# The GLA heads of a two-layer streaming step: SyncE's transfers in the source's order, the first gates and the samples' values asked later

## The chip, the core and the metric

The kernel runs on one core of one Trainium2 chip. The metric is the device time of one execution in microseconds (us). The core has five engines with a queue of instructions each, executed in order: TensorE (PE, matrix products), ScalarE (ACT), VectorE (DVE), GpSimd (POOL) and SyncE (SP), which only issues transfers. Transfers (DMA) are issued by SP, ACT and POOL and carried by 16 shared DMA engines; the profile names the queues of the three q1 (SP), q10 (ACT) and q0 (POOL). An instruction waits for semaphores that others raise, and whatever stands behind it on its engine waits too.

## The reference

Two layers act on 512 prompt frames and on 8 running streams of 16 frames each, 640 frames of 2048 channels together. The first is stick-breaking attention; the second, which matters here, is gated linear attention (GLA) with four heads. In float32, for chunks of a head:

```python
def gla_chunk(S, inp):
    q, k, v, g = inp
    C = q.shape[1]
    b = jnp.cumsum(g, axis=1)
    b_last = b[:, -1]
    q_in = q * jnp.exp(b)
    a = jnp.einsum('bchd,bshd->bhcs', q_in, k * jnp.exp(-b))
    a = jnp.where(jnp.tril(jnp.ones((C, C), dtype=bool)), a, 0.0)
    o = jnp.einsum('bhcs,bshe->bche', a, v) + jnp.einsum('bchd,bhde->bche', q_in, S)
    S = jnp.exp(b_last)[..., None] * S + jnp.einsum('bshd,bshe->bhde', k * jnp.exp(b_last[:, None] - b), v)
    return S, o

def gla_mixer(h, w_in, w_a2, b_a, g_out, w_out, S0=None):
...
    q, k, v, r, a_lr = jnp.split(h @ w_in, [nk, 2 * nk, 2 * nk + nv, 2 * nk + 2 * nv], axis=-1)
...
    g = (jax.nn.log_sigmoid((a_lr @ w_a2 + b_a).astype(f32)) / GLA_TAU).reshape(B, T, GLA_HEADS, GLA_DK)
...
    o = o * lax.rsqrt(jnp.mean(o * o, axis=-1, keepdims=True) + EPS) * g_out.astype(f32).reshape(GLA_HEADS, GLA_DV)
    y = (o.reshape(B, T, nv) * jax.nn.silu(r.astype(f32))).astype(h.dtype) @ w_out
    return y, S.astype(h.dtype)
```

For the streams S0 is the given state; the new states are outputs.

## The kernel before

Every float32 product is made of three reduced ones: a weight piece `wr` (128x1024, 512 KB) is cast by ACT to `wh` (L134) and the rest is subtracted by DVE to `wl` (L135), and PE multiplies wh, wh and wl with the two halves of the activations. Weights are read once, from HBM, with two raw buffers in flight, so a piece is asked for when ACT and DVE have emptied the buffer that it takes.

The change touches one stage, "layer 1's heads" (the block that opens at L1508). Five pieces of work run in it beside one another:

- `plain` (L632) makes q and k of heads 1 to 3 from the normed input: a unit is 48 matmuls of 128x320 with one weight piece, two units make a block of 128 channels, and `keep` (L1513) copies the block's two halves out of PSUM by ACT (`pl`, L1519) and stores it by ACT's queue to `gq` or `gk` in HBM (L1521). There are two PSUM banks for it, so a half can begin only when the copy of that half of the block before is done.
- `decays` loads a head's q and k back (`load`, L71, by SP) and makes the decay factors on ACT and DVE.
- `prompt_lane` runs 16 chunks (4 heads of 4): scores, the product with the values `v` (fetched two chunks ahead from `gv` in HBM, two pairs of buffers), the state S, the norm, and the multiplication by the output gate (`gate`, fetched from `gr`, GP buffers), whose result ACT stores to `og` (L1610). When that store is issued, the gate that will take the same buffer is asked after a delay.
- `sample_lane` does the streams: 64 states of 256 KB go in and out by POOL's queue (`move`, L78), and for every head its values are brought by SP (`v`) and POOL (`vst`).
- `fetches` loads the finished `og` rows back (`og_in`) and splits them; `share` (L686) multiplies them with the output weights, its first products copied out by ACT (`y`, L708) and later ones added by DVE (L705).

Which of these comes next is decided while the program is written: a planner counts PE's time ("pe now", in us) and steps the pieces; `side.after(t, f)` calls f when t us of PE's time have gone by. That gives the source's order. The order in which an engine's queue gets its instructions is then made by a scheduler, from times that it estimates, over all engines; only dependences bind it. So SP's transfers before the change stand in the scheduler's order and not in the source's. Each transfer of SP and ACT takes the next of eight semaphores in turn, and one that takes a semaphore waits until the transfer that had it before has landed.

Of the kernel before, what the change touches and what calls it, by code (L numbers as in the profile page):

```python
# [34 lines left out]
GP = 2  # L35
# [6 lines left out]
def hybrid_step_kernel(ctx: ExitStack, tc: tile.TileContext, A: dict, O: list):  # L42
# [106 lines left out]
    def wraw(src, a, n):  # L149
        r = wp.tile([P, 1024], F32, tag="wr", name="wr", bufs=WR)[:, :a * n]  # L150
        load(r.rearrange("p (a n) -> p a n", a=a), src)
        return r
# [121 lines left out]
    def step(wait=0.0, tp=0, z=0, tiled=False):  # L274
        return wait, tp, z, tiled
# [70 lines left out]
    side = Side()  # L346
# [569 lines left out]
    with tc.tile_pool(name="kp", bufs=2, reuse_waits="tile") as kp, \  # L916
# [297 lines left out]
        for x in (prompt_lane(0), prompt_lane(1), sample_lane()):  # L1214
            side.add(x)
# [287 lines left out]
    def w_of(g, c, i):  # L1503

        k0 = 4 * g + 2 * i
        return w_out1.rearrange("(kt p) n -> p kt n", p=P)[:, k0:k0 + 2, 512 * c:512 * c + 512]

    with tc.tile_pool(name="gl", bufs=1, reuse_waits="tile") as gl, \  # L1508
            tc.tile_pool(name="w4", bufs=1, reuse_waits="tile") as w4:
        came = {"plain": False, "last": False, "of": 0, "when": 0.0}  # L1510

        def keep(dst, hh):
# [78 lines left out]
        def gate(h, t0, tag, bufs):  # L1591
            g = gl.tile([P, 4, P], F32, tag=tag, name="gate", bufs=bufs)
            load(g, gr_d[h][:, :, t0:t0 + P])
            return g
# [7 lines left out]
        def leave(h, t0, on, g, then):  # L1602

            tp = bank("tp")
            for s in range(4):
                turn_block(tp[:, P * s:P * s + P], block(on[:, P * s:P * s + P]), ident)
            dve.tensor_tensor(g, tp.rearrange("p (s t) -> p s t", s=4), g, op=ALU.mult)

            def out():
                nc.scalar.dma_start(out=og_d[h][:, :, t0:t0 + P], in_=g)  # L1610
                then()
            side.after(2.0, out)
# [66 lines left out]
        def prompt_lane():  # L1679
# [7 lines left out]
            def fetch_gate(u):  # L1687
                if u < len(units):
                    gs[u] = gate(units[u][0], P * units[u][1], "gp", GP)
# [1 line left out]
            fetch(0)  # L1691
            side.after(10.0, lambda: fetch(1))
            for u in range(GP):
                side.after(14.0 + 2.0 * u, lambda u=u: fetch_gate(u))
            left = None

            def state(S, e1, dt, c):
# [7 lines left out]
            def leave_left():  # L1705
                nonlocal left
                u, on = left
                left = None
                h, c = units[u]

                def then():
                    side.after(7.0, lambda: fetch_gate(u + GP))
                    if c == 3:
                        through["p"] = h + 1
                leave(h, P * c, on, gs.pop(u), then)
# [94 lines left out]
        def sample_lane():  # L1810
            def fetch(h):
                v = values(h, 4, "vn", 1)

                for e in range(2):
                    for i in range(3):
                        rows = gv_d[h][int(i == 1)][NP:, :].rearrange("(m e t) n -> e t m n", m=4, e=2)[e]
                        r0 = 64 * e + NT * i
                        move(vst[r0:r0 + NT].bitcast(F32), rows)
                return v, gate(h, NP, "gn", 1)

            yield step(12.0)
            here = fetch(0)
            for h in range(GH):
                v, g = here
# [134 lines left out]
        for x in (decays(), prompt_lane(), sample_lane(), fetches()):  # L1959
            side.add(x)  # L1960
# [8 lines left out]
        parts = [split(r) for r in first]  # L1969
        first = [wraw(w_of(3, 0, i), 2, 512) for i in range(2)]  # L1970
        side.finish()


    share_banks(mm=8)
# [96 lines left out]
```

## Time and profile before

| | |
|---|---|
| median of three runs | 2514.42 us (2511.73 to 2514.44) |
| the profiled execution | 2514.76 us, its span 2513.0 us |
| mean granted clock of PE | 0.984 |
| the stage of the change | about 1979 to 2395 us of the span |
| PE's idle time before matmuls of `plain` (L654, wh) | 8.8 us, of it 6.3 for ACT's copy pl |
| transfers in the whole run | 503.12 MB, mean 200 GB/s |
| of it by SP, POOL, ACT | 441.85, 41.43 and 17.04 MB |

A row of a timeline has the start in the span (us), the length (us), the engine, the line of the kernel, the operation, out<-in by the program's names, the shape, how many instructions are drawn together, and in brackets how long the engine stood before it and what released it. SPq and ACTq are the issues of transfers on these engines: their length is that of the issue, or of the stretch over several, and not of the transfer. A row of waits has the engine and line, what it waited for, the us in total, how often, and the longest. A row of a DMA queue has its packets, MB and share of the 16 engines' time in the window. A row of the chain of waits has the start, the length and what the time went to.

The share of DMA time in the stage changes much: in windows of 20 us it is 1.01 from 1980 (303 GB/s), 0.66 from 2000, 0.54 from 2020, 1.00 from 2080, 0.49 from 2120 and 1.03 from 2240 (373 GB/s).

### The profile page before, as it was taken

To read this page: it belongs to the slowest core of one execution; us is meant where nothing else is said; L and a number is where in the kernel's file an instruction comes from. 1 tells how busy PE (TensorE), PEld (TensorE's weight loads), DVE (VectorE), ACT (ScalarE), POOL (GpSimd) and SP (SyncE) were. 2 spreads that over 40 slices of the span, in tenths; PEclk is the share of its full clock that TensorE was granted. 3 is DMA by queue.
4 is the path that set the end of the run, shared out by engine and by line. 5 is a ranking of instruction groups with operands and counts; after the bars stand their busy time and mean duration, and the time that the engine had idled before them with its cause. 6 is when DMAs were issued, how large, how long until landed. Compare 5 with 4: busy or idle time off the path is not lost.

```text
span 2513.0 us, 43986 instructions
## 1 busy us (share of the span) xinstructions
PE 2427.7 (97%) x17561; PEld 2150.1 (86%) x17561; DVE 1580.6 (63%) x2566; ACT 994.1 (40%) x1731; POOL 135.2 (5%) x350
## 2 busy tenths in 40 slices
PE   6899999999999999999999999999999999999998
PEld 4589999899999998888887767999999989987776
DVE  5575555555666655666776568766676466675556
ACT  4332222222223334555544245333333455565223
POOL 0010000000000000000000000000000212332000
PEclk8899999999999999999999999999999999999999
DMA  9966666667664357777874664443534758976634
GB/s 343 330 210 216 224 205 208 221 214 226 209 202 126 110 166 227 256 243 236 259 235 146 187 226 134 129 118 110 145 104 117 209 183 271 294 265 218 226 114 147
DMA packets 487502, 503.12 MB, mean 200 GB/s; under 512 B 42746, under 2 KB 387202, under 8 KB 487170
## 3 DMA queue, kind: packets, MB, share of 16 engines
q1 hardware_dynamic: 456978, 441.85, 55.8%
q0 software_dynamic: 12848, 41.43, 4.8%
q10 hardware_dynamic: 17472, 17.04, 2.0%
q8 instruction: 138, 2.26, 0.4%
q14 instruction: 66, 0.54, 0.1%
HBM read 411.10 MB, written 89.13 MB: 199 GB/s over the span
## 4 chain that ended last, share of the span: by engine, by line
PE 78%; DMA 6%; DVE 4%; ACT 3%; issue 1%; SPq 0%; POOL 0%; ACTq 0%; POOLq 0%; DVEq 0%
PE ps_mm L595 40%; PE ps_mm L700 9%; PE ps_mm L654 9%; PE ps_mm L369 3%; PE ps_tp L1086 2%; DMA gv<-kr 2%; PE ps_tp L1559 2%; PE ps_mm L519 1%; PE ps_tp L1046 1%; PE ps_tp L1138 1%; PE ps_z L1022 1%; PE ps_z L180 1%; PE ps_mm L2042 1%; PE ps_z L1100 1%; PE ps_z L222 1%
## 5 line engine op out<-in xcount | busy, mean ns | idle before, releaser
L595 PE MATMUL ps_mm<-sums,wh 128*128 128x320 f32 x2752 | 613.5, 311 | 1.5 <-ACT wh L134 1.5
L595 PE MATMUL ps_mm<-h,wh 128*128 128x320 f32 x2064 | 462.8, 312 | 4.7 <-DVE u L601 4.7
L595 PEld LDWEIGHTS ps_mm<-sums,wh 128*128 128x128 f32 x2752 | 457.9, 188 | 10.4 <-issue 7.4
L595 PE MATMUL ps_mm<-sums,wl 128*128 128x320 f32 x1376 | 425.3, 309 | 0.7 <-DVE wl L135 0.7
L135 DVE TENSOR_TENSOR wl<-wr,wh 128x1024 fp32r<-128x1024 f32 x193 | 236.1, 1224 | 232.3 <-ACT wh L134 228.9
L595 PEld LDWEIGHTS ps_mm<-h,wh 128*128 128x128 f32 x2064 | 344.0, 188 | 20.7 <-issue 14.6
L134 ACT CAST wh<-wb 128x1024 fp32r<-128x1024 f32 x170 | 178.4, 1050 | 426.5 <-PE ps_mm L595 350.3
L134 ACT CAST wh<-wr 128x1024 fp32r<-128x1024 f32 x193 | 202.5, 1050 | 329.3 <-PE ps_mm L595 186.7
L595 PE MATMUL ps_mm<-h,wl 128*128 128x320 f32 x1032 | 319.3, 309 | 0.0
L654 PE MATMUL ps_mm<-h,wh 128*128 128x320 f32 x1152 | 265.7, 318 | 8.8 <-ACT pl L1519 6.3
L595 PEld LDWEIGHTS ps_mm<-sums,wl 128*128 128x128 f32 x1376 | 258.3, 188 | 1.0 <-DVE wl L135 1.0
L135 DVE TENSOR_TENSOR wl<-wb,wh 128x1024 fp32r<-128x1024 f32 x170 | 207.8, 1223 | 62.7 <-ACT wh L134 62.5
L654 PEld LDWEIGHTS ps_mm<-h,wh 128*128 128x128 f32 x1152 | 193.7, 190 | 23.5 <-issue 8.9
L700 PE MATMUL ps_mm<-wh,ogh 128*128 128x512 f32 x450 | 197.3, 438 | 7.2 <-ACT y L708 4.0
L595 PEld LDWEIGHTS ps_mm<-h,wl 128*128 128x128 f32 x1032 | 194.2, 188 | 0.0
L654 PE MATMUL ps_mm<-h,wl 128*128 128x320 f32 x576 | 178.8, 310 | 0.0
L700 PE MATMUL ps_mm<-wl,ogh 128*128 128x512 f32 x450 | 177.2, 394 | 0.3 <-DVE wl L135 0.3
L700 PE MATMUL ps_mm<-wh,ogl 128*128 128x512 f32 x450 | 177.2, 394 | 0.3 <-DVE ogl L135 0.3
L700 PEld LDWEIGHTS ps_mm<-wh,ogh 128*128 128x128 f32 x450 | 85.0, 189 | 35.7 <-issue 14.3
L654 PEld LDWEIGHTS ps_mm<-h,wl 128*128 128x128 f32 x576 | 109.1, 189 | 0.2 <-DVE wl L135 0.2
L700 PEld LDWEIGHTS ps_mm<-wh,ogl 128*128 128x128 f32 x450 | 84.7, 188 | 20.3 <-DVE ogl L135 0.7
L519 PE MATMUL ps_mm<-wh,h 128*128 128x512 f32 x252 | 93.2, 431 | 5.7 <-ACT h L134 3.7
(359 smaller groups left out, 3712.9 us busy)
## 6 DMA issues: line engine op xcount, KB each, us to landing
ar<-in_w_ada_dram SPq DMA_DIRECT2D x160, 512.0 KB
wb<-in_sb_w_in_dram SPq DMA_DIRECT2D x82, 512.0 KB
kc<-in_cache_sb_k_dram SPq DMA_DIRECT2D x64, 512.0 KB
vc<-in_cache_sb_v_dram SPq DMA_DIRECT2D x64, 512.0 KB
wr<-in_gla_w_in_dram SPq DMA_DIRECT2D x51, 512.0 KB
wb<-in_gla_w_in_dram SPq DMA_DIRECT2D x45, 512.0 KB
wr<-in_sb_w_in_dram SPq DMA_DIRECT2D x44, 512.0 KB
ar<-in_w_ada_dram SPq DMA_DIRECT2D x64, 256.0 KB
```

The lines of the kernel that those rows point to most:

```text
L134: nc.scalar.copy(hi, x)
L135: (e or dve).tensor_tensor(lo, x, hi.bitcast(F32), op=ALU.subtract)
L180: mm(acc[32 * q:32 * q + 32, :w], cT[:, kt + m, :], by(cT[:, kt + m, :], rs[m // each][:, m % each, q, :]), start=kt + m == 0, stop=kt + m ...
L222: mm(acc[32 * j:32 * j + 32, :256], cT[:, kt + m, :], by(cT[:, kt + m, :], r[:, 256 * j:256 * j + 256]), start=kt + m == 0, stop=kt + m == ...
L369: mm(acc[a], l[:, c], by(l[:, c], r[:, k2, :]), start=kt == k0 and first, stop=kt == k0 + nk - 1 and last)
L519: mm(acc[a], l, by(l, r[:, e, :]), start=j == 0 and e == 0 and begun, stop=j == 7 and e == 1 and last)
L595: mm(acc, l[:, k, :], by(l[:, k, :], r), start=start and k == 0 and first, stop=k == 7 and last, skip_group_check=True)
L654: mm(acc[nt], l[:, k, :], by(l[:, k, :], r), start=k0 == 8 and k == 0 and first, stop=k0 == 0 and k == 7 and last)
L700: mm(acc, l, by(l, r[:, e, :]), start=i == 0 and e == 0 and first, stop=i == 1 and e == 1 and last)
L1022: mm(z[:, :n], q[:, hh, qs], by(q[:, hh, qs], k[:, hh, :n]), start=True, stop=True)
L1086: turn_block(tp[:, P * c:P * c + P], block(kc[:, c, P * hh:P * hh + P]), ident)
L1559: mm(out, l[a], by(l[a], r[b]), start=start and n == 0, stop=stop and n == 2, skip_group_check=True)
```

## The change

Four edits, all in the heads' stage:

- SP's queue is taken from the scheduler for the length of the stage (`manual_schedule` for the engine SP): its transfers are issued in the order in which the source asks for them. The other engines' queues are still the scheduler's.
- The first GP gates are asked at 40, 44, ... us of the planner's clock instead of 14, 16, ...
- A gate that refills a buffer is asked 6 us after the store that frees it, instead of 7.
- The samples' lane begins at 30 us instead of 12, and with it its values are asked later.

```diff
@@ -1507,6 +1507,8 @@
     with tc.tile_pool(name="gl", bufs=1, reuse_waits="tile") as gl, \
             tc.tile_pool(name="w4", bufs=1, reuse_waits="tile") as w4:
+        loads = ExitStack()
+        loads.enter_context(tc.manual_schedule(engines={mybir.EngineType.SP}))
         came = {"plain": False, "last": False, "of": 0, "when": 0.0}
@@ -1691,7 +1693,7 @@
             for u in range(GP):
-                side.after(14.0 + 2.0 * u, lambda u=u: fetch_gate(u))
+                side.after(40.0 + 4.0 * u, lambda u=u: fetch_gate(u))
@@ -1709,7 +1711,7 @@
                 def then():
-                    side.after(7.0, lambda: fetch_gate(u + GP))
+                    side.after(6.0, lambda: fetch_gate(u + GP))
@@ -1818,7 +1820,7 @@
-            yield step(12.0)
+            yield step(30.0)
             here = fetch(0)
@@ -1969,6 +1971,7 @@
         side.finish()
+        loads.close()
```

The rest is told by the order of the rows on each engine, in which a row is the line, the operation, out<-in and the shape. PE's rows stand in the same order before and after. Those of ACT, DVE and POOL move a little; POOL's moves `vst` keep their place among its transfers. SP's rows move much. Lines of the changed kernel are 2 higher in this stage.

The first place is the beginning of the stage on SP, from the first pair of values on, about 1982 us of the span; `-` is before and `+` the change:

```order
 L71 DMA v<-gv_0_107 128x512
 L71 DMA v<-gv_1_108 128x512
+L71 DMA wr<-in_gla_w_in_dram 128x8x128
 L71 DMA q<-gq_95 128x1280
 L71 DMA k<-gk_99 128x1280
+L71 DMA wr<-in_gla_w_in_dram 128x8x128
 L71 DMA v<-gv_0_107 128x512
 L71 DMA v<-gv_1_108 128x512
+L71 DMA wr<-in_gla_w_in_dram 128x8x128 x2
 L71 DMA v<-gv_0_107 128x512
 L71 DMA v<-gv_1_108 128x512
-L71 DMA gate<-gr_103 128x4x128 x3
```

Two weights that stood ahead of these rows now stand among them, two more came forward from behind the gates, and the three gates are now asked one by one, later.

The second place is SP about 2086 to 2102 us, before:

```order
L71 DMA gate<-gr_104 128x4x128
L71 DMA og_in<-og_91 128x384
L71 DMA wa_21838<-wa_d 96x256
L71 DMA wr<-in_gla_w_in_dram 128x8x128
L71 DMA gate<-gr_104 128x4x128
L71 DMA wr<-in_gla_w_in_dram 128x8x128
```

and now:

```order
L71 DMA gate<-gr_104 128x4x128
L71 DMA wr<-in_gla_w_in_dram 128x8x128
L71 DMA gate<-gr_104 128x4x128
L71 DMA wr<-in_gla_w_in_dram 128x8x128
L71 DMA wa_21840<-wa_d 96x256
L71 DMA wr<-in_gla_w_in_dram 128x8x128
```

The second gate is the same in both. The weight that stood ahead of it (with wa) now stands behind it, and the weight that is now ahead of it was asked earlier still, outside these rows.

The third place is about 2238 to 2262 us, where the output weights and the og rows are brought; SP before:

```order
L71 DMA wr<-in_gla_w_out_dram 128x2x512
L71 DMA og_in<-og_92 128x640
L71 DMA v<-gv_1_114 128x512
L71 DMA v<-gv_0_113 128x512
L71 DMA wr<-in_gla_w_out_dram 128x2x512
L71 DMA k<-gk_102 128x1280
L71 DMA og_in<-og_92 128x640 x2
L71 DMA gate<-gr_106 128x4x128 x2
L71 DMA og_in<-og_92 128x640
L71 DMA wr<-in_gla_w_out_dram 128x2x512 x2
```

and now:

```order
L71 DMA wr<-in_gla_w_out_dram 128x2x512 x2
L71 DMA q<-gq_98 128x1280
L71 DMA k<-gk_102 128x1280
L71 DMA og_in<-og_92 128x640 x2
L71 DMA gate<-gr_106 128x4x128
L71 DMA og_in<-og_92 128x640
L71 DMA gate<-gr_106 128x4x128
L71 DMA wr<-in_gla_w_out_dram 128x2x512 x2
```

q of the last head (asked near 2192 before) now stands here, and the weight that stood ahead of k is the first of the last row, behind both gates and three og rows.

ACT at the same place, about 2260 to 2268 us, before (the first row is the cast of that weight):

```order
L134 CAST wh<-wr 128x1024
L1651 ACTIVATE b<-b 128x640
L708 COPY y<-ps_mm 128x512
L1652 ACT_TABLE_LOAD
L1652 ACTIVATE b<-b 128x640
L1848 CAST kc<-kd 128x4x32
L1610 DMA og_93<-gate 512x1x128
L708 COPY y<-ps_mm 128x512
L1661 ACT_TABLE_LOAD
```

and now:

```order
L1612 DMA og_93<-gate 512x1x128
L708 COPY y<-ps_mm 128x512
L134 CAST wh<-wr 128x1024
L1663 ACT_TABLE_LOAD
L1663 ACTIVATE e_23482<-b 128x4
L1664 ACTIVATE el<-b 128x4
L1666 ACTIVATE es<-b 128x8
L1669 ACTIVATE ed<-ed 128x4
L708 COPY y<-ps_mm 128x512
```

The cast of the same weight has moved from ahead of the second decay's steps to between the copy and the table load, with the next copy y six rows behind it.

## The prediction

> **What bounds the kernel now.** First the page, for the share of TensorE (PE), then PE's waits in the stage that the change touches, 1960 to 2400 us of the span.
>
> ```profile
> PE 2427.7 (97%) x17561; PEld 2150.1 (86%) x17561; DVE 1580.6 (63%) x2566; ACT 994.1 (40%) x1731; POOL 135.2 (5%) x350
> ```
> ```profile
> PE ps_mm L654 <- ACT pl L1519: 6.3, 1, 6.3
> PE ps_mm L700 <- ACT y L708: 3.8, 2, 1.9
> ```
>
> PE is busy 97% of the span, so only its waits can be won, and in this stage they are few: 6.3 us once, for a copy of ScalarE (ACT) that frees a bank, and 3.8 us in two waits for other copies of ACT. PE's own order is the same before and after; the change acts only through the loads of SyncE (SP). The ACT timeline and the chain of waits show where the 6.3 us come from.
>
> ```profile
> 1986.96 1.05 ACT L134 CAST wh<-wr 128x1024 fp32r<-128x1024 f32 x1 [1.12 <-PE ps_mm L654]
> 1990.63 0.43 ACT L1519 COPY pl<-ps_mm 128x320 f32<-128x320 f32 x1 [2.62 <-PE ps_mm L654]
> ...
> 2002.59 0.33 ACTq L1521 DMA_DIRECT2D gq<-pl  x1
> 2002.95 1.28 ACT L1651 ACT_TABLE_LOAD   x1 [7.00 <-DMA v<-gv]
> ```
> ```profile
> 1986.01 16.50 DMA v<-gv
> ```
>
> ACT stood 7.00 us until a load of values (issued 1986.01, 16.50 us under way) had landed. What waited was the store gq<-pl at the head of its queue: the eight semaphores of SP's and ACT's transfers go round, and the one that the store got was held by that load. Behind it stood the decays and the copy that PE wanted. The PE timeline gives the price.
>
> ```profile
> 2015.08 0.90 PE L654 MATMUL ps_mm<-h,wh 128*128 128x320 f32 x2 [6.26 <-ACT pl L1519]
> ...
> 2018.38 0.45 PE L654 MATMUL ps_mm<-h,wh 128*128 128x320 f32 x2
> 2018.82 0.46 PE L654 MATMUL ps_mm<-h,wh 128*128 128x320 f32 x2
> ```
>
> PE stood 6.26 us. The 12 matmuls from 2015.08 to 2018.38 then took 3.30 us; three take 0.44 us at the full clock (2018.38 to 2018.82), so 1.76 us: 1.54 us more are lost to the slower clock. **The place costs 7.8 us in all.**
>
> The other side of the stage is its transfers. Of the DMA view I read three windows: 1983 to 1997 (its row of SP's queue, q1), 2089 to 2102 (GpSimd's queue q0, then q1) and 2239 to 2255 (q1).
>
> ```profile
> q1 hardware_dynamic: 865, 2.28, 52.8%
> ```
> ```profile
> q0 software_dynamic: 825, 2.56, 60.5%
> q1 hardware_dynamic: 1615, 0.97, 24.7%
> ```
> ```profile
> q1 hardware_dynamic: 1101, 2.62, 45.8%
> ```
>
> Beside GpSimd's states SP's queue moved 2.28 MB in 14 us (0.163 MB/us) and 2.62 MB in 16 us (0.164) where it held long packets too, but 0.97 MB in 13 us (0.075) where it held mostly short ones, as a weight is. These are my two prices for a load that has to land in such a stretch.
>
> **The change part by part.** *The store (−7.8).* In the new order the store's semaphore belongs to the first pair of values, asked some 2 us earlier and with far less ahead of them; ACT's wait of 7.00 us goes, and the 6.26 and 1.54 us with it. What is late next is a weight. SP's timeline:
>
> ```profile
> 1967.31 10.89 SPq L71 DMA_DIRECT2D wr<-in_gla_w_in_dram  x3
> 1978.63 3.08 SPq L74 DMA_DIRECT2D gr<-out  x2
> 1981.81 0.37 SPq L71 DMA_DIRECT2D alr_in<-alr_d  x1
> 1982.23 0.43 SPq L71 DMA_DIRECT2D wa<-wa_d  x1
> 1982.71 1.84 SPq L71 DMA_DIRECT2D v<-gv  x2
> ```
>
> *Third and fourth weight (+5.4).* Before, three weights were asked by 1978.2. Now one is; the next (cast at 1986.96 before) follows the two v, at about 1984.6, into GpSimd's burst of states. Ahead of its end in SP's queue, from 1981.4: one gr 320, alr 240, wa 96, two v 512 and itself 512, 1.68 MB. At 0.163 MB/us from 1983 it lands at 1993.3; with its own 512 KB at 0.075 at 1997.0. I take the middle, 1995.2. Then the cast (1.05) and VectorE's subtraction, by its group on the page:
>
> ```profile
> L135 DVE TENSOR_TENSOR wl<-wr,wh 128x1024 fp32r<-128x1024 f32 x193 | 236.1, 1224 | 232.3 <-ACT wh L134 228.9
> ```
>
> 1.22 us. It is usable at 1997.5, and ACT's copy of 1990.63, which stands behind that cast, is late too. PE wants both when the unit that began at 1986.9 ends: 48 matmuls of 0.147 us and two of the decays, 1994.2. PE stands 3.0 us (0 to 5). The fourth weight follows q and k (1.28 MB): 1.79 MB more at 0.163 would be 2006.2, somewhat sooner as the states end near 2000; usable about 2006.8, against 1994.2 + 3.0 + 7.2 = 2004.4: 2.4 us (0 to 4). Net of this first place: −7.8 + 5.4 = **−2.4** (−7.8 to +1).
>
> *First gates, samples' values, delay of 6.0: nothing.* GpSimd's moves of the samples' values keep their place in its order, so that part hardly exists. The gates' cover is long:
>
> ```profile
> 2052.74 1.03 SPq L71 DMA_DIRECT2D v<-gv  x2
> 2056.61 0.54 SPq L71 DMA_DIRECT2D gate<-gr  x1
> ```
> ```profile
> 2060.27 1.05 ACT L134 CAST wh<-wr 128x1024 fp32r<-128x1024 f32 x1 [0.17 <-PE ps_mm L654]
> ```
>
> The gate of 2056.61 refills the buffer of the first one used, so that one was used just before; asked up to 25 us later it is still there 20 us ahead. Without that cover every us late would be a us of VectorE's queue.
>
> *Weights behind values, 2050 to 2090 (+2, 0 to 6) and 2140 to 2230 (+1.5, 0 to 5).* In source order a weight stands behind the pair of values asked before it, which waits until PE has freed their buffers. So the weight of the cast of 2060.27 is asked at 2053.8, behind the pair of 2052.74; its 512 KB take 3.1 to 6.8 us and some start, so ACT may wait 0 to 2 us with PE's copy behind it. The same once more near 2086, and at some four weights later; most keep several us of slack.
>
> *Behind a gate (+4, 0 to 9).*
>
> ```profile
> 2088.48 0.55 SPq L71 DMA_DIRECT2D wr<-in_gla_w_in_dram  x1
> 2101.44 0.54 SPq L71 DMA_DIRECT2D gate<-gr  x1
> 2102.07 0.65 SPq L71 DMA_DIRECT2D wr<-in_gla_w_in_dram  x1
> ```
> ```profile
> 2102.60 1.05 ACT L134 CAST wh<-wr 128x1024 fp32r<-128x1024 f32 x1 [1.04 <-PE ps_mm L654]
> 2103.56 0.42 ACT L1519 COPY pl<-ps_mm 128x320 f32<-128x320 f32 x1
> ```
>
> The weight of 2088.48 now stands behind the gate of 2101.44, which waits for a store of ACT. Gate and weight are 768 KB: landed at 2106.2 by 0.163 MB/us, at 2111.7 by 0.075. ACT still has that cast ahead of the copy of 2103.56, which comes 1.5 us after the landing, 2107.7 to 2113.2. PE wants it half a unit after 2102.6, at about 2106.5: a wait of 1.2 to 6.7 us; the middle is 4.
>
> *The output rows' place (+5, 0 to 9).* SP, the chain, then ACT:
>
> ```profile
> 2239.91 1.16 SPq L71 DMA_DIRECT2D wr<-in_gla_w_out_dram  x1
> ```
> ```profile
> 2244.91 10.53 DMA og_in<-og
> ```
> ```profile
> 2267.32 1.28 ACT L1661 ACT_TABLE_LOAD   x1
> ...
> 2270.32 0.57 ACT L708 COPY y<-ps_mm 128x512 f32<-128x512 f32 x1
> ```
>
> The weight of 2239.91 moves behind two other weights, q, k, three og_in and two gates. The third og_in needs a buffer that is free only when the first has landed and been split. Two weights, q, k and that og_in are 2.62 MB from about 2239: at 0.164 MB/us landed near 2255.5 (before: the 10.53 us of 2244.91 end at 2255.4); cast and split bring 2257, the second og_in and the gate's wait SP to about 2260. Then 256 + 320 + 256 + 512 KB, 1.34 MB, lie up to the weight's end: 8 us at 0.164, 18 at 0.075; I take 13, near the first, as half of it is long packets: 2273. ACT's new order has the cast right ahead of the table load of 2267.32 and the copy of 2270.32 behind both, so that copy slips 5 to 6 us, and PE waits for it.
>
> *The tail of the stage (+2.5 and +2.5, 0 to 4 each).* SP and ACT:
>
> ```profile
> 2313.36 0.53 SPq L71 DMA_DIRECT2D gate<-gr  x1
> 2326.06 1.08 SPq L71 DMA_DIRECT2D og_in<-og  x2
> 2328.10 7.75 SPq L71 DMA_DIRECT2D wr<-in_gla_w_out_dram  x2
> ```
> ```profile
> 2330.67 1.53 ACT L134 CAST ogh<-og_in 128x640 fp32r<-128x640 f32 x2 [1.89 <-DMA og_in<-og]
> ```
>
> Two weights asked long before now stand behind the gate of 2313.36, and ACT meets the first at about 2316, so a landing near 2319 to 2321 holds the copies behind it 2 to 4 us. The og_in of 2326.06, for which ACT waits already (1.89), goes behind the weight of 2328.10: 2 us later asked and 512 KB further back. Some of each is lost in waits that are there now.
>
> **The sum**: −2.4 + 2 + 4 + 1.5 + 5 + 2.5 + 2.5 = +15.1 us. The profiled execution took 2514.76 us, 1.8 over its span of 2513.0 and 0.34 over the median of 2514.42: 2529.9, say **2530**.
>
> The slower clock was seen once, behind 6.26 us of idle PE (3.30 us for 12 matmuls). The Trainium skill, page "TensorE: Matmul & The Clock Gate", section "What's actually happening", has the half clock after an idle window of about 3.4 us; by that the new waits of 4 and 5 us would cost 1.54 us each as well, 2533. The sum is without it.
>
> **The rivals.** *Only the store's wait goes* (faster): 2514.8 − 7.8 = **2507**. It needs each weight to land before ACT reaches its cast, at the first place before 1992. For it speak the many us of slack of most weights; against it that five places fail together only if SP's queue gets much more than 0.163 MB/us beside GpSimd's.
>
> *SP lags with PE* (no change): where PE stands, all that asks for loads also comes later, and the prices past 2230 aren't paid: −2.4 + 2 + 4 + 1.5 = +5 at most, **2517** with half of them. Against it: gates wait for stores and og_in for a split, not for PE alone.
>
> *One packet each* (slower still): in 2089 to 2102 q0 had 825 packets and q1 1615; were they one for one while both are full, q1 would get 825 of 0.6 KB, 0.038 MB/us. Then gate and weight of 2101.44 take 20 us instead of the 5 to 10, that place costs 15 more; I take 11, as q0 is empty for part of the time: **2541**. The trace's two to one speaks half against it. The Trainium skill, page "DMA: Bandwidth & Descriptors", section "Queues, rings and completion order", says that each DMA engine takes turns between its queues packet by packet, which is this case.
>
> *The order isn't changed where it matters*: excluded by the listing of SP's rows.
>
> **How the numbers follow.** Forecast 0.47, one packet each 0.2, SP lags 0.17, only the store 0.16. The range runs from 2509 to 2546: all new waits at their low end would be 2507, all at the high end 2552, and neither is likely whole. About 0.2% (5 us) can be told from no change: faster 0.16, same 0.17, slower 0.67.
>
> **What would show it.** Right: the wait of ACT's store is gone; PE waits of 2 to 4 us near 1994 and 2004 behind casts of wr; one of some 4 us near 2107 for pl (L1519); one of 5 to 7 near 2270 for y (L708); SP waits for ACT's og stores with weights behind them. Wrong: if no ACT cast waits for a load of wr, the first rival holds; if PE waits appear at other engines' work (states of GpSimd, VectorE's gate), my list of places is wrong even where the sum fits.

## The result, and the profile after

| | kernel before | changed kernel |
|---|---|---|
| median (runs, lowest to highest), us | 2514.25 (6, 2511.73 to 2516.75) | 2532.51 (6, 2527.07 to 2546.49) |
| ratio, 95% interval | 1 | 1.0084 [1.0067, 1.0101] |
| profiled execution (its span), us | 2514.76 (2513.0) | 2534.39 (2532.7) |
| mean granted clock of TensorE | 0.984 | 0.982 |

The change costs 18.3 us by the medians. The page of the changed kernel, in its rows for the engines and for the matmuls of `plain` with wh on TensorE (PE) (duration in all, ns of one, idle time before them and what ended it), and below them the same kernel's waits of PE from 1960 to 2420 us:

```profile
PE 2433.7 (96%) x17561; PEld 2155.1 (85%) x17561; DVE 1580.2 (62%) x2566; ACT 993.8 (39%) x1731; POOL 134.4 (5%) x350
L654 PE MATMUL ps_mm<-h,wh 128*128 128x320 f32 x1152 | 268.6, 320 | 11.8 <-ACT pl L1521 8.7
```
```profile
PE ps_mm L654 <- ACT pl L1521: 8.7, 3, 5.9
PE ps_mm L700 <- ACT y L708: 8.6, 3, 4.3
PE ps_tp L1856 <- DVE kc L1851: 3.1, 2, 2.0
PE ps_tp L1649 <- DMA wa<-wa_d: 1.1, 1, 1.1
```

Before, the first two were 6.3 and 3.8 us. PE's busy time rose too, from 2427.7 to 2433.7 us for the same 17561 matmuls. Where that happened is seen by cutting both spans at the same matmuls (those at 1978, 2230 and 2400 us of before). A row gives the window, its length, PE's busy time in it (and how many matmuls), the mean granted clock, and the transfers' share and GB/s. The kernel before, then the changed one:

```profile
1978.00:2230.00 252.00, 245.01 (x1579) 0.99 0.79 248
2230.00:2400.00 170.00, 163.22 (x757) 1.00 0.69 230
```
```profile
0.00:1973.60 1973.60, 1912.16 (x14783) 0.99 0.62 195
1973.60:2238.70 265.10, 250.88 (x1578) 0.97 0.73 230
2238.70:2419.70 181.00, 167.65 (x758) 0.96 0.67 227
```

From 1978 to 2230 (called the front below) the change costs 13.1 us, of which 5.9 are slower matmuls; from 2230 to 2400 (the tail) 11.0, of which 4.4 are slower matmuls. So of 24.1 us, 13.8 are waiting and 10.3 are a lower clock. Ahead of the stage, where both kernels do the same, this execution was 4.4 us quicker than that of before (1973.6 for 1978.0, 4.2 of it busy time at a clock of 0.99 for 0.98): that is no effect of the change, and it makes 19.7 us of the span out of 24.1 in the stage.

**Weights come late, as copies of ScalarE (ACT) behind their casts show.** The changed kernel's first place, by the timelines of SP, ACT and PE (start, duration, engine, and in brackets the idle time before it and what ended it):

```profile
1978.68 1.12 SPq L71 DMA_DIRECT2D v<-gv  x2
1979.89 1.11 SPq L71 DMA_DIRECT2D wr<-in_gla_w_in_dram  x1
```
```profile
1993.78 1.04 ACT L134 CAST wh<-wr 128x1024 fp32r<-128x1024 f32 x1 [6.66 <-DMA wr<-in_gla_w_in_dram]
1994.73 0.42 ACT L1521 COPY pl<-ps_mm 128x320 f32<-128x320 f32 x1
```
```profile
1995.20 0.90 PE L654 MATMUL ps_mm<-h,wh 128*128 128x320 f32 x2 [2.64 <-ACT pl L1521]
```

The weight is asked behind the pair of values and lands 13.9 us later; ACT stands 6.66 us at its cast, and the copy that frees PE's bank stands behind it. The second place, near 2105 of before, where a gate waits for a store of ACT at the head of SP's queue:

```profile
2094.52 0.53 SPq L71 DMA_DIRECT2D gate<-gr  x1
2095.16 0.90 SPq L71 DMA_DIRECT2D wr<-in_gla_w_in_dram  x1
```
```profile
2084.91 0.52 ACTq L1612 DMA_DIRECT2D og<-gate  x1
2107.03 1.04 ACT L134 CAST wh<-wr 128x1024 fp32r<-128x1024 f32 x1 [9.85 <-DMA wr<-in_gla_w_in_dram]
```
```profile
2108.45 0.90 PE L654 MATMUL ps_mm<-h,wh 128*128 128x320 f32 x2 [5.93 <-ACT pl L1521]
```

The place near 2270 of before shows as the chain of work in the changed kernel (start, duration, what): the split of a row of og, SP, the weight behind it, its cast, a table load, the copy y, PE.

```profile
2268.69 0.83 DVE ogl L135
...
2269.53 0.33 SPq L71
...
2270.55 10.14 DMA wr<-in_gla_w_out_dram
...
2280.71 1.05 ACT wh L134
...
2281.78 1.28 ACT L1663
```

And the one at the end of the tail, SP, ACT and PE:

```profile
2313.89 14.58 SPq L71 DMA_DIRECT2D gate<-gr  x2
2328.56 1.23 SPq L71 DMA_DIRECT2D wr<-in_gla_w_out_dram  x2
```
```profile
2336.04 1.05 ACT L134 CAST wh<-wr 128x1024 fp32r<-128x1024 f32 x1 [4.92 <-DMA wr<-in_gla_w_out_dram]
```
```profile
2340.95 0.80 PE L700 MATMUL ps_mm<-wh,ogh 128*128 128x512 f32 x1 [4.26 <-ACT y L708]
```

**Behind each of these waits the clock is down.** Windows of the changed kernel that begin right behind the waits of 2.64, 5.93, 2.03 (for kc), 2.34 and 4.26 us; the number behind the count is the mean granted clock:

```profile
1996.00:2003.00 7.00, 6.97 (x31) 0.61 0.84 272
2108.40:2114.00 5.60, 5.55 (x19) 0.50 0.70 250
2247.00:2252.00 5.00, 4.87 (x18) 0.66 0.83 243
2284.00:2290.00 6.00, 5.90 (x20) 0.72 0.69 266
2340.90:2347.00 6.10, 6.05 (x19) 0.56 0.72 247
```

### The profile page after: what moved, and what is told of

Read it like the earlier page. It is cut to its first block, busy times and chain, and to the rows that moved or that the text cites. A ratio compares the mean times of both kernels' runs of the same rounds, so it can differ in the third digit from the quotient of the medians.

```text
span 2532.7 us, 43970 instructions
## 1 busy us (share of the span) xinstructions
PE 2433.7 (96%) x17561; PEld 2155.1 (85%) x17561; DVE 1580.2 (62%) x2566; ACT 993.8 (39%) x1731; POOL 134.4 (5%) x350
## 4 chain that ended last, share of the span: by engine, by line
PE 78%; DMA 7%; DVE 4%; ACT 3%; issue 2%; POOL 0%; ACTq 0%; SPq 0%; POOLq 0%; DVEq 0%
PE ps_mm L595 39%; PE ps_mm L700 9%; PE ps_mm L654 8%; PE ps_mm L369 3%; PE ps_tp L1086 2%; PE ps_tp L1561 2%; DMA gv<-kr 1%; PE ps_mm L519 1%; PE ps_tp L1046 1%; PE ps_tp L1138 1%; PE ps_z L180 1%; PE ps_z L1022 1%; DMA wr<-in_gla_w_in_dram 1%; PE ps_mm L2045 1%; PE ps_z L1100 1%
## 5 line engine op out<-in xcount | busy, mean ns | idle before, releaser
L595 PEld LDWEIGHTS ps_mm<-h,wh 128*128 128x128 f32 x2064 | 343.0, 188 | 19.9 <-issue 15.1
L654 PE MATMUL ps_mm<-h,wh 128*128 128x320 f32 x1152 | 268.6, 320 | 11.8 <-ACT pl L1521 8.7
```

Source lines behind the costliest of these rows:

```text
L595: mm(acc, l[:, k, :], by(l[:, k, :], r), start=start and k == 0 and first, stop=k == 7 and last, skip_group_check=True)
L654: mm(acc[nt], l[:, k, :], by(l[:, k, :], r), start=k0 == 8 and k == 0 and first, stop=k0 == 0 and k == 7 and last)
```

## The experiments

Each kernel differs from before or from the changed kernel as its diff says. Front and tail are how much later a kernel runs through 1960 to 2230 and 2230 to 2400 us of before, by the start of the same matmul (counted along PE's order) in its trace and in before's; since they are from one execution each, and the stretch ahead of 1960 was 2.3 to 8.6 us quicker in all of them than in that of before, in most of the slower ones they sum to more than the medians show. e6_front keeps SP's order of the change in the front and lost 4.6 us less there, so single figures of front and tail are good to some us only.

| kernel | median (runs) | before beside it | ratio [95%] | front | tail |
|---|---|---|---|---|---|
| the change | 2532.51 (6) | 2514.25 | 1.0084 [1.0067, 1.0101] | +13.1 | +10.9 |
| e1_delays | 2513.98 (10) | 2512.08 | 1.0012 [1.0001, 1.0022] | +0.5 | +1.4 |
| e2_order | 2535.68 (4) | 2512.08 | 1.0097 [1.0082, 1.0112] | +18.7 | +9.8 |
| e6_front | 2523.86 (4) | 2512.08 | 1.0056 [1.0040, 1.0072] | +8.5 | +4.6 |
| e6_tail | 2523.96 (4) | 2512.08 | 1.0053 [1.0038, 1.0068] | +2.6 | +12.6 |
| e3_gate14 | 2528.50 (4) | 2510.74 | 1.0066 [1.0050, 1.0083] | +14.0 | +7.6 |
| e9_early_front | 2510.39 (11) | 2510.74 | 0.9999 [0.9990, 1.0009] | -2.3 | +2.9 |
| e10_tail_early | 2523.21 (5) | 2510.74 | 1.0040 [1.0023, 1.0056] | +1.1 | +11.2 |
| e10_all_early | 2523.26 (6) | 2510.74 | 1.0040 [1.0026, 1.0054] | -1.3 | +14.6 |
| e7_poolstore | 2510.61 (12) | 2511.78 | 0.9995 [0.9987, 1.0004] | -1.4 | -0.2 |
| e11_pool_og | 2513.29 (11) | 2511.78 | 1.0007 [0.9996, 1.0017] | -3.0 | +4.1 |
| e11_front_pool_og | 2508.07 (12) | 2511.78 | 0.9988 [0.9980, 0.9997] | -2.9 | -0.6 |
| e12_after_pool_og | 2527.99 (6) | 2511.73 | 1.0061 [1.0048, 1.0074] | +13.0 | +10.5 |

### Which part of the change costs

The three delays alone, on the kernel before (e1_delays):

```
-                side.after(14.0 + 2.0 * u, lambda u=u: fetch_gate(u))
+                side.after(40.0 + 4.0 * u, lambda u=u: fetch_gate(u))
...
-                    side.after(7.0, lambda: fetch_gate(u + GP))
+                    side.after(6.0, lambda: fetch_gate(u + GP))
...
-            yield step(12.0)
+            yield step(30.0)
```

> The kernel before with only the three delays of the change (first gates at 40 + 4u, refill after 6.0, samples' lane from 30), SP's queue left to the scheduler. Theory 'order' (the loss comes from SP's source order, in which weights stand behind gates, values and og rows): no loss, 2506 to 2516 us; the first values' pair of the samples and three gates leave the burst of 1986 to 1996, so the 6.3 us wait for ACT's copy may shrink. Theory 'delays' (gates and values asked later are what costs): 2525 to 2535 us, with DVE waiting for gates.

The source's order alone, with the delays of before (e2_order: the same three lines turned back in the changed kernel):

> The changed kernel with the old delays (14 + 2u, 7.0, 12.0): SP's source order alone. Theory 'order': at least the loss of the change, 2530 to 2545 us, somewhat more than the change, since the early gates and the samples' values now stand ahead of the third and fourth weight, so that PE waits some 5 us more at 1994 to 2010. Theory 'delays': 2510 to 2516 us.

The source's order up to the end of the projections only (e6_front), and from there on only (e6_tail):

```
         drive(others)
+        loads.close()
```
```
         drive(others)
+        loads = ExitStack()
+        loads.enter_context(tc.manual_schedule(engines={mybir.EngineType.SP}))
         for g in range(2):
```

> The changed kernel with SP's source order ended where the q and k products end (about 2230 us), the output weights' part again in the scheduler's order. In the profiled execution of the change PE lost 13.1 us up to 2230 against before and 10.9 behind it. Theory 'each place by itself': the front's loss stays and the tail's goes, 2523 to 2530 us, the waits for y (L708) back at two of 2 us. Theory 'shift' (the tail is late only because the front is): 2532 us or so, as the change.

> The other half: SP's source order only from the end of the q and k products on, with the change's delays. Theory 'each place by itself': 10.9 us of the tail on top of the kernel with the delays alone, 2520 to 2528 us, PE waits for y (L708) of 2 to 5 us behind casts of wr near 2280 and 2335. Theory 'shift': as before, 2510 to 2516 us.

The delays alone cost 1.9 us, at the edge of what can be told; the order alone costs 23.6. So the order is the cause. Both halves keep the new delays: they cost 11.8 and 11.9, which with the delays' 1.9 counted once is 21.8, beside the 18.3 of the change (16.8 to 25.4 by its interval). So either side of 2230, put into the source's order alone, costs about as much as the other.

The two tails aren't the same loss, though. In e6_tail 9.3 of its 12.6 us go between 2250 and 2260 of before, where the change loses 1.5: ACT stands there until an earlier store of gated rows has landed (issued 2234.27, 15.67 us under way).

```profile
2250.59 0.53 ACT L1648 ACTIVATE b<-ps_tp,cols 128x320 f32<-128x320 f32 x1 [9.17 <-DMA og<-gate]
```

From 2225 to 2420 ACT waits for no such store in the change, nor in e2_order and e3_gate14. It does in e6_tail, e10_tail_early and e10_all_early, whose tail is in the source's order and whose front was on time (-1.3 to +2.6 us). So e6_tail doesn't tell by what the change's own tail loses its time.

And the delays aren't nothing beside the new order. In e2_order the first place, from 1978 to 2020 of before, costs 6.0 us where it costs the change 0.3. The third weight is late in both; but in e2_order ACT's store of q stands for a load of values again, as before, and the cast behind it comes late to the matmul that had waited 6.26 us (PE waits 2.28 for wh there and 0.70 for wl):

```profile
2001.75 1.28 ACT L1653 ACT_TABLE_LOAD   x1 [4.75 <-DMA v<-gv]
```

The medians point the same way (23.6 and 18.3 us over before), though the intervals of the ratios overlap.

### Is it the gate at the head of the queue?

The changed kernel with gates refilled 8 us later, which was to let the store that they wait for land first (e3_gate14):

```
-                    side.after(6.0, lambda: fetch_gate(u + GP))
+                    side.after(14.0, lambda: fetch_gate(u + GP))
```

> The change with the refill of a gate asked 14 us after its store instead of 6, so that SP meets a store that has landed. Theory 'head of the queue' (a gate that waits for its store holds the weight behind it): the loss of 8.8 us near 2105 falls below 2, that near 2340 may stay, in all 2521 to 2529 us. Rival 'share of the queue' (the weight is late because SP's packets get little beside GpSimd's): 8 us stay at 2105, 2530 to 2534 us.

The loss near 2105 went from 8.7 us to nothing. But the edit did something else than it was meant to: the gate still stands at the head of SP's queue until its store has landed (SP waits 27.7 us in three for such stores from 2080 to 2120, 15.7 in two in the change), only now the weight of that place is ahead of it:

```profile
2088.61 0.38 SPq L71 DMA_DIRECT2D wr<-in_gla_w_in_dram  x1
...
2098.68 0.53 SPq L71 DMA_DIRECT2D gate<-gr  x1
```

So the weight's place behind a gate that waits is what cost the 8.7 us. The total hardly fell: the same kernel lost 5.8 us between 2050 and 2104, where the change lost nothing, and 9.1 from 2140 to 2230 against 4.5. Two of its waits of PE that the change did not have, the second for VectorE's product with the gate, which now comes late (L1609):

```profile
PE ps_tp L1884 <- ACT on L1590: 3.1, 1, 3.1
PE ps_tp L1884 <- DVE gate L1609: 2.0, 1, 2.0
```

The place also depends on how long the transfers are under way. In e6_front SP has the same order there, but ACT's store (issued 2085.55) let the gate go at 2091.53, and weight and cast followed as below (SP, then ACT); ACT waited 4.11 us and not 9.85, and PE 0.2 for the copy and not 5.93; from 2050 to 2118 of before this kernel lost 2.3 us in all, in small waits.

```profile
2092.15 0.56 SPq L71 DMA_DIRECT2D wr<-in_gla_w_in_dram  x1
```
```profile
2101.35 1.05 ACT L134 CAST wh<-wr 128x1024 fp32r<-128x1024 f32 x1 [4.11 <-DMA wr<-in_gla_w_in_dram]
```

### Are late weights the cause?

The source's order, but each weight of the q and k products asked one piece earlier, so that two are under way (e9_early_front is e6_front with this; the tail is the scheduler's), in the buffers that `wr` has already:

```
+        ahead = piece(2) if early else None
...
-                    nxt, raw = second if n == 0 and second else (wsplit(raw, 8), piece(n + 2))
+                    if early:
+                        nxt, raw, ahead = wsplit(raw, 8), ahead, piece(n + 3)
+                    else:
+                        nxt, raw = second if n == 0 and second else (wsplit(raw, 8), piece(n + 2))
```

> The front alone in source order, as in e6_front (2523.9 us), but the source asks each weight of the q and k products one piece earlier, as soon as the split of the piece that holds its buffer is asked for: the same order of all else, gates and values where they were. Theory 'late weights': the front's loss goes and the first wait of 7.8 us, too, does not come back or only partly, 2507 to 2514 us; SP waits for DVE's wl instead. Rival 'gates and values' (their own lateness, or SP's waits for stores, hold PE): 2519 to 2525 us.

The front's loss of 8.5 us became a gain of 2.3, and the ratio went from 1.0056 to 0.9999; ACT's waits for weights from 1965 to 2232, 23.6 us in six in the change, are one of 3.0. **In the front it is the late weights.**

The same for the output weights in the tail, with the front left to the scheduler (e10_tail_early is e6_tail with this), and both together on the whole change (e10_all_early):

```
+        def then(c, i):
+            if early and c < 4:
+                raws.append(raw(c, i))
...
-            if c < 3:
+            if c < 3 and not early:
                 raws += [raw(c + 1, 0), raw(c + 1, 1)]
...
                     w0 = made()
+                    then(c + 2, 0)
```

> The tail alone in source order, as in e6_tail (2524.0 us), but the source asks each output weight as soon as the split of the piece that holds its buffer is asked for. Theory 'late weights': of the tail's some 11 us at least half goes, 2514 to 2519 us, and the wait for y of 6.8 us near 2255 falls below 3. Rival 'og rows' (og_in, q and k in one burst hold ACT): 2521 to 2526 us.

> The whole change with both kinds of weights asked one piece earlier. Theory 'late weights': the sum of the two, 2510 to 2518 us, at most 0.2% from before. Rivals of the two runs above: 2525 us or more.

Here the theory failed: 2523.21 where late weights alone would have given 2514 to 2519, and a tail of +14.6 in e10_all_early. The weight near 2270 no longer cost anything in e10_tail_early (-1.3 us from 2260 to 2280, where e6_tail lost 2.8), but the place near 2250 cost 10.0, as it had cost e6_tail 9.3. In e10_all_early it is again ACT, by its timeline, and the chain there shows for what it stood:

```profile
2247.31 0.54 ACTq L1624 DMA_DIRECT2D og<-gate  x1
2247.90 0.53 ACT L1662 ACTIVATE b<-ps_tp,cols 128x320 f32<-128x320 f32 x1 [8.33 <-DMA og<-gate]
```
```profile
2233.72 13.51 DMA og<-gate
```

ACT's store of gated rows waited to be issued until an earlier store of ACT had landed, 13.51 us after its issue, among the two weights, q, k and two og_in that SP issued at 2233.6 to 2237.9. Behind it in ACT's queue stood the copies that free PE's banks. It is the pattern of the first place of before, a store that stands at the head of ACT's queue until another transfer has landed.

### ACT's stores

The test: from about 2230 on, the gated rows are stored by GpSimd's queue and not by ACT's. On the whole change with early weights (e11_pool_og), on e9_early_front (e11_front_pool_og) and on the changed kernel itself (e12_after_pool_og):

```
-                nc.scalar.dma_start(out=og_d[h][:, :, t0:t0 + P], in_=g)
+                (nc.gpsimd if came["plain"] else nc.scalar).dma_start(out=og_d[h][:, :, t0:t0 + P], in_=g)
```

> The kernel with the whole change and both groups of weights asked a piece earlier (2523, +14.6 us between 2230 and 2400), with one difference: from the end of the projections on (about 2230) the stores of the gated rows (og<-gate) are issued by POOL in place of ACT. Theory 'in the tail ACT stands at its own store, for which a semaphore is held by a transfer in SP's burst': ACT's wait of 8.3 us in front of the activation b (2239 to 2247) goes, and with it 7 to 9 us of the tail: 2513 to 2517. Theory 'SP's order itself is late there (rows of og and weights behind gates)': the loss moves to a wait for og_in or wr by ACT, 2520 to 2526. POOL's stores stand between its state transfers; where one waits for VectorE's gate, states come later: up to +4.

> The kernel with SP in source order up to about 2230 and the weights of the q and k products asked a piece earlier, the scheduler's order behind it (2510.4, equal to before), with the same difference: og<-gate issued by POOL from about 2230 on. There ACT did not stand at that store; its tail lost 2.9 us to rows of og (ACT waits for og_in 5.7 and 1.5 us). If these rows only stood behind ACT's late stores: 2505 to 2509, faster than before. If the store on ACT was never late here: 2509 to 2513, the same. If POOL's states come later: up to 2515.

> The changed kernel itself, weights asked where the change asks them, with one difference: og<-gate is issued by POOL in place of ACT from about 2230 on. Its front (1960 to 2230) stays as the change has it, about +13 us by the time of the matmuls. Theory 'the tail's loss comes from ACT's late stores of og, behind which gates, rows of og and with them weights stand in SP's order': the tail falls from +10.9 to +2 to +5 us, 2524 to 2527. Theory 'the tail's weights are late by their place in SP's order alone': the tail stays at +8 to +11 (waits for y, L708, at 2268 and 2320), 2529 to 2533. If only the earlier weights make the stores on POOL useful (both are needed): +6 to +9, 2527 to 2530.

With early weights the store was it: ACT's wait of 8.33 us is gone, the tail fell from +14.6 to +4.1, and the ratio from 1.0040 to 1.0007. These stores were also under way for less, by the DMA view of e11_pool_og from 2230 to 2247 (count, KB of each, median us to landing):

```profile
og<-gate POOLq DMA_DIRECT2D x2, 256.0 KB, 7.1
```

On the changed kernel itself the same edit did little: 1.0061 [1.0048, 1.0074] beside 1.0084 [1.0067, 1.0101], intervals that overlap, and a tail of +10.5 in its profile (of the slowest of its six runs). That is what the change's trace lets expect, since its ACT waits for no such store; the weights still came late (PE waits for y of 7.9 us in four). How much late weights are worth in the changed kernel's own tail isn't settled. Less the place of ACT's store (8.8 us of e10_all_early, 9.3 of e6_tail) the tails are 5.8 us with early weights and 3.3 with late ones, both behind a front that was on time, against 10.9 in the change.

e11_front_pool_og is the fastest of all, 0.9988 [0.9980, 0.9997]. Beside it e11_pool_og, which differs only in the tail's order and its weights, is 5.2 us slower by the medians: the source's order in the tail still costs about that with both mended.

The last test is of the stall that the prediction saw as the whole of the gain: the kernel before, with the stores of q and k (dst<-pl) on GpSimd's queue, so that ACT doesn't stand at them (e7_poolstore):

```
-                    nc.scalar.dma_start(out=dst[:, hh, :], in_=t[0])
+                    nc.gpsimd.dma_start(out=dst[:, hh, :], in_=t[0])
```

> The kernel before, with one difference: the stores of q and k to HBM (dst<-pl) are issued by GpSimd (POOL) in place of ScalarE (ACT), so that they take semaphores of another set and ACT never stands at one. Theory 'the store's semaphore is the first stall': ACT's 7.00 us and PE's 6.26 us near 2009 to 2015 go (with the 1.54 of the slow clock, 7.8 in all at most); SP's order stays, so what the change lost at weights is not paid; if nothing else is late at that place -4 to -8 us: 2504 to 2508. Theory 'the stall is PE's slack and comes back at the next wait' (the change's own trace had the 7.8 back within 30 us): -2 to 0, 2510 to 2512. If POOL's stores now stand behind its state transfers and q or k comes late to the decays, a new wait of 1 to 5 us near 1995: 2511 to 2517.

ACT's wait of 7.00 us is gone, but the place is only 1.7 us shorter (2.6 won at PE's wait, 0.9 lost at one 6 us later), and the time is 0.9995 [0.9987, 1.0004]. PE, then ACT of this kernel:

```profile
2004.52 0.56 PE L654 MATMUL ps_mm<-h,wh 128*128 128x320 f32 x2 [3.65 <-ACT pl L1519]
```
```profile
2000.72 1.04 ACT L134 CAST wh<-wr 128x1024 fp32r<-128x1024 f32 x1 [4.32 <-PE ps_mm L654]
2001.67 0.73 ACT L1671 ACTIVATE y<-b 128x640 f32<-128x640 f32 x1
2002.44 0.94 ACT L1648 ACTIVATE b<-ps_tp,cols 128x320 f32<-128x320 f32 x2
2003.42 0.74 ACT L1651 ACTIVATE b<-b 128x640 f32<-128x640 f32 x1
2004.06 0.41 ACT L1519 COPY pl<-ps_mm 128x320 f32<-128x320 f32 x1
```

With the store out of the way the copy still stands behind three activations of the decays and a cast that itself waits 4.32 us for PE: PE still waits 3.65 us of its 6.26.

## Why the prediction was right

It said 2530 (2509 to 2546), slower, and 2532.51 came. In the front the cause is the one that it named, weights that are asked behind values and gates and that ACT casts ahead of copies that PE waits for: e9_early_front shows it. In the tail the traces show the same at two weights and a late row of og, but no run takes these away alone. That the number came so close is in part luck: in the stage the two traces differ by 24.1 us where the sum had 15.1. The steps fared unevenly; the measured numbers are by the start of the same matmul.

- *The store's stall and the two weights behind it* (-7.8 and +5.4, net -2.4): -8.1 and +8.4, net **+0.3**, inside its range of -7.8 to +1. The old stall went whole in the change, though e7_poolstore shows that the store alone was worth only about 1.7 of it, and in e2_order, with the order alone, a part of it stays. The third weight was usable later than worked out: landed at 1993.75, which is 1998.2 in before's time, against 1993.3 to 1997.0. It cost 2.9 us at PE's wait (2.64), near the 3.0 that was said, and 3.1 of clock behind it. The other 2.4 went just ahead, with PE's waits for ACT's cast of h (0.49) and for the load of wa (1.14), and aren't the weight's. The fourth weight, for which 2.4 was said, cost nothing.
- *First gates, samples' values, delay* (nothing): next to nothing alone (e1_delays, +1.9 us with the interval's lower end at 1.0001), but with the new order they keep the old stall away: the first place costs some 6 us more without them (e2_order's trace beside the change's, one execution each). The sum had put that at nothing.
- *Weights behind values, 2050 to 2090* (+2): nothing was lost there; 0 was the low end. *2140 to 2230* (+1.5, 0 to 5): **4.5**, but some 2.5 of it by the mechanism of the next item: ACT stands 4.64 us for a weight at 2204.89 that SP issued behind a gate, for whose store it had waited 14.9 us. The rest is small waits.
- *Behind a gate* (+4, 0 to 9): **8.7**, the place and the chain as written, at the top of its range. Gate and weight, 768 KB, took 12.4 us from the gate's issue at 2094.52, 0.062 MB/us, less than the lower of the two prices (0.075). In e6_front the same pair took 9.8.
- *The output rows' place* (+5): the chain is there link by link, but cost **2.0** by 2280 of before (2.34 of wait, and the slow clock, less what was lost there before): its weight landed at 2280.69, near 2268 in before's time, and not at 2273. The 13 us taken for that weight were the middle of 8 and 18, and not "near the first"; 10.14 were measured from issue to landing. *The tail's end*: **4.7** at the weight behind the gate, for which 2.5 was said, and nothing at og_in, for which 2.5 was said too.
- Not in its list: 3.3 us near 2235 to 2240 of before, a wait of PE for VectorE's kc behind a late row of og, and 1.5 near 2255.

The step that was missing is the clock. The prediction held that only PE's waits can be won or lost, priced the new ones at their length and took 1.54 us off for the old stall; the stage lost 10.3 us to slower matmuls. Waits alone came to +13.8 where the sum had +16.6 (its +15.1 without the -1.54): they were taken somewhat too long. Together the two errors leave the sum 9 us short of the stage's 24.1. Of these, 4.4 come back ahead of the stage, where that execution was sooner; the medians differ by 18.3, 3 us more than was said. The rule that the prediction set beside its sum, from the Trainium skill, page "TensorE: Matmul & The Clock Gate", section "What's actually happening", gave 2533 with a slower clock behind the waits of 4 and 5 us; the trace bears it out in kind. In size the trace goes further: the clock fell behind waits of 2.03 and 2.34 us too, shorter than the 3.4 us that the page states for its window.

Of the rivals, *only the store's wait goes* needed every weight to land before its cast: ACT stands for weights at each place. *SP lags with PE* needed the places past 2230 to cost nothing: they cost 10.9. *One packet each* would have had the gate and weight near 2105 take 20 us: they took 12.4.

## What to carry to other kernels

An order of loads is worth what it does to the loads behind the ones that wait: when a queue is put into the source's order, look first for loads that stand behind one that waits for a buffer or a store, and ask those earlier by a buffer; here that alone made the front's order free. Before a loss of one half is taken for a half of the whole loss, see in its trace that it stands at the same waits. A wait that is removed is worth only the time until the next thing in that engine's queue is late, so trace what stands behind it before counting it whole. And where the matrix engine stands, add the slow matmuls after the wait to the wait: here 10.3 us beside 13.8.

## What the runs showed of the hardware that was not expected

- TensorE's mean granted clock was 0.50 to 0.72 over the 5 to 7 us behind waits of 2.03 to 5.93 us (the five windows above). Cut narrower, it was 0.50 behind the waits of 2.03 and 2.34 us for some 3.3 us (2247.3 to 2250.6 and 2284.9 to 2288.1) and around the ends of the other three for some 6.5 (1994.8 to 2001.4, 2107.5 to 2114.0 and 2339.5 to 2346.2), and 1.00 right behind each. In the first place 21 matmuls of 0.147 us took 6.17 us in place of 3.1.
- The same 256 KB store of gated rows by ACT was under way for 9.6 us (issued 2084.91, its gate's load behind it issued 2094.52), and for 13.51 and 15.67 us in SP's burst (e10_all_early, e6_tail); from GpSimd's queue in that burst (e11_pool_og) it took 7.1.
- The stretch ahead of the stage, the same work in every kernel, differed by up to 8.6 us from one profiled execution to another. One profile beside another tells nothing of differences of that size unless they are read stage by stage.
